# One decode step of 16 attention heads: from split products with 128 stationary columns to plain fp32 products with 32, in column groups of the array

## The chip, the core and the metric

The kernel runs on one core of one Trainium2 chip. The metric is the device time of one execution in microseconds. TensorE (PE) multiplies, with a separate instruction that loads the stationary operand (PEld); VectorE (DVE), ScalarE (ACT) and GpSimd (POOL) do elementwise work; SyncE (SP) issues most transfers.

## The reference, cut to what matters

One layer of a hybrid streaming encoder is computed for a prompt of 512 tokens and for 8 decode sequences of 16 tokens, all in fp32. Head group A has 16 heads of 64. Its decode part, which is what the change touches, is plain attention over a cache of 256 keys and the 16 new ones, with a learned bias by relative distance:

```python
s = jnp.einsum('bgqhrd,bgkhd->bghrqk', q, k) * (HEAD_DIM ** -0.5)
s = s + bias
p = jnp.exp(s - m); denom = jnp.sum(p, axis=-1, keepdims=True)
w = (p / denom).astype(v.dtype)
o = jnp.einsum('bghrqk,bgkhd->bgqhrd', w, v)
```

Around it stand the input projections, the prompt's attention, group B's attention, an output projection and a gated feed-forward network of 2048 x 5632.

## The kernel before, in words

All tokens (512 + 128 = 640) are columns, in two halves of 320. Large products are **dense**: a weight tile of 128 x 128 stays in the array and 320 columns pass through it. An fp32 operand is split into a high part (fp32r, by ACT) and a low rest (by DVE), and a product becomes three: high by high, high by low, low by high (`mm3`, lines 207 to 209 for all callers). Products that stay plain fp32 stand on lines 251 and 263 (row sums and a broadcast for the norms). Transposes are TensorE instructions on line 324.

Attention is written as generators. `decode_a(g)` treats the 8 heads of half g as four pairs of heads; one pair's queries are the 128 rows (two heads of 64). For each of the 8 batch elements b it

1. places the element's queries in `z`, whose other places are zero, so that in the 128 stationary columns of pair t only the 32 columns of that pair (2 heads x 16 tokens) are filled;
2. loads the keys (`cka`), splits them and adds them into one bank with three products for each of four pairs, all accumulating, since the zeros keep the pairs apart: 12 products of 272 columns;
3. adds the bias, takes maximum and exponent (ACT, lines 699 and 700), and loads the values (`cva`);
4. transposes the probabilities of 128 rows (3 transposes), splits them, splits the values and multiplies all 512 value columns by all 128 query rows: 3 x 3 products of 512 columns. Of those 512 columns a row needs only its own head's 64;
5. scales by the denominator, transposes 4 blocks and copies the wanted diagonal blocks out (`diagonal`).

Order of work. `pump` advances one generator by one `yield`; `tick` calls it at a given rate after each step of a dense product (6 matmuls). From the fifth pair of projections on there are two streams, heads of the prompt and `decode` (group B's decode, then `decode_a(0)`), which take turns; `drain_queue("decode")` after the last projection pumps until both parts are done. Then group B's attention outputs are read back and scaled (`group_operands`, lines 202 and 203) as operands of the first output projection, into whose 16 dense products `decode_a(1)` is fed. The number of yields in `decode_a` therefore decides over how many dense steps it spreads. TensorE runs the recorded order (`keep_pace`); other engines' orders come from a scheduler. Buffers S, W and D are slots handed out in turn (`get`, `put`).

Of the kernel before, what the change touches and what calls it, by code (L numbers as in the profile page):

```python
# [7 lines left out]
AF = mybir.ActivationFunctionType  # L8
ALU = mybir.AluOpType
# [4 lines left out]
P = 128  # L14
D = 2048
# [6 lines left out]
NB = 8  # L22
DS = 16
CA = 256
# [17 lines left out]
def f(ap):  # L42
    return ap.bitcast(F32)
# [250 lines left out]
def diagonal(ap, first):  # L294

    return bass.AP(tensor=ap.tensor, offset=ap.offset + first, ap=[list(ap.ap[0]), [160, 4], [1, DS]])


def r(ap):
    return ap.bitcast(F32R)  # L300


def build(nc, tc, io, pools):
    n = Net(nc, tc, io, pools)
    dma = nc.sync.dma_start
# [14 lines left out]
    def dram(name, shape):  # L320
        return pools["dr"].tile(list(shape), F32, tag=name, name=name)

    def tr(out, src):
        nc.tensor.transpose(out, src, n.ident)  # L324
# [12 lines left out]
    oa_d, ob_d = dram("oa_d", (8, P, TOK)), dram("ob_d", (8, P, TOK))  # L337
    sa_d, sb_d = dram("sa_d", (3, P, 8, P)), dram("sb_d", (P, 8, P))
# [14 lines left out]
    first = []  # L353
    for kt in range(KT):
# [10 lines left out]
        own, hl = pair("S")  # L365
# [83 lines left out]
    def flip(blocks, lst):  # L449
        w = P * len(blocks)  # L450
        ps = n.bank()[:, :w]
        for i, src in enumerate(blocks):
            tr(ps[:, P * i:P * i + P], src)
        if w <= HT:
            own = (n.get(lst),)
            hl = pack(own[0], w)
        else:
            own, hl = pair(lst, w)
        n.split(ps, *hl)
        return own, hl  # L460
# [183 lines left out]
        n.put("D", kb0, kb1, vb0, vb1)  # L644

    def decode_a(g):
        o_s, bias, z = n.get("D"), n.get("D"), (n.get("D"), n.get("D"))
        for w in z:
            nc.gpsimd.memset(w, 0.0)
        dma(out=bias[:, :CA + DS], in_=io["bias_d"][g])  # L650
        new, held = [], []
        for i in range(3):
            s, two = n.get("S"), (n.get("D"), n.get("D"))
            sv, hl = sh(s, 4, P), [r(sh(x, 4, P)) for x in two]
            dma(out=sv, in_=sa_d[i, :, 4 * g:4 * g + 4])
            yield
            if i < 2:
                n.split(sv, *hl)
            else:
                ps = n.bank().rearrange("p (a b) -> p a b", a=4)  # L660
                for j in range(4):
                    tr(ps[:, j], sv[:, j])
                n.split(ps, *hl)
            n.put("S", s)
            held.extend(two)
            new.append(hl)
        qh, kh, vh = new
        for b in range(NB):
            own = slice(DS * b, DS * b + DS)
            for e in range(2):  # L670
                zv = r(sh(z[e], 4, 160))
                for rr in range(2):
                    rows = slice(64 * rr, 64 * rr + 64)
                    nc.vector.tensor_copy(zv[rows, :, DS * rr:DS * rr + DS], f(qh[e])[rows, :, own])
            raws = n.get("S"), n.get("S")
            for hf in range(2):
                dma(out=sh(raws[hf], 2, CA), in_=io["cka"][b, g, hf])
            yield
            ps = n.bank()[:, :CA + DS]
            for hf in range(2):  # L680
                ko = n.get("S"), n.get("S")
                kd = [r(sh(x, 2, CA + DS)) for x in ko]
                n.split(sh(raws[hf], 2, CA), kd[0][:, :, :CA], kd[1][:, :, :CA])
                n.put("S", raws[hf])
                for e in range(2):
                    nc.gpsimd.tensor_copy(kd[e][:, :, CA:], f(kh[e])[:, 2 * hf:2 * hf + 2, own])
                yield
                yield
                for j in range(2):
                    t = 2 * hf + j  # L690
                    n.mm3(ps, [r(z[e][:, P * t:P * t + P]) for e in range(2)],
                          (kd[0][:, j], kd[1][:, j]), t == 0, t == 3)
                n.put("S", *ko)
# [5 lines left out]
            nc.scalar.activation(pt[:, :CA], s[:, :CA], AF.Exp, bias=mx, accum_out=den)  # L699
# [12 lines left out]
            yield  # L712
            po = n.bank()
            for j in range(2):
                two, vd = pair("S", 512)
                n.split(raws[j][:, :512], *vd)
                n.put("S", raws[j])
                yield
                yield
                n.mm3(po, cut(p3, P * j, P * j + P), vd, j == 0, False)  # L720
                n.put("S", *two)
            n.mm3(po, cut(p3, 256, 384), [x.rearrange("p a b -> p (a b)") for x in vh], False, True)
            n.put("S", *own3)
            od = n.get("S")
            nc.vector.tensor_scalar(od[:, :512], po, den, None, ALU.mult)
            yield
            yield
            pf = n.bank()
            for t in range(4):
                tr(pf[:, P * t:P * t + P], od[:, P * t:P * t + P])  # L730
            n.put("S", od)
            for rr in range(2):
                rows = slice(64 * rr, 64 * rr + 64)
                nc.vector.tensor_copy(sh(o_s, 4, P)[rows, :, own], diagonal(pf[rows], DS * rr))
        dma(out=oa_d[4 * g:4 * g + 4, :, SP:].rearrange("t p c -> p t c"), in_=sh(o_s, 4, P))
        n.put("D", o_s, bias, *z, *held)


    kf, vf = n.get("F"), n.get("F")
# [18 lines left out]
    ps = n.bank()[:, :P]  # L758
# [38 lines left out]
    for p in range(8):  # L797
        if p < 4:
            project_b(2 * p)
            project_b(2 * p + 1)  # L800
        if p == 4:
            while len(n.lists["Q"]) < 4:
                n.pump()
            n.put("S", kb2, kb3)
            n.move("Q", "D", 4)
            n.put("D", cos, sin)
            n.streams = (("heads 0", "heads"), ("decode", "decode"))
            n.add("decode", decode_b())
            n.add("decode", decode_a(0))
            n.rate = 1.1  # L810
        project_a(p)
# [83 lines left out]
    for i, m in enumerate(m for kt in range(8) for m in (kt, kt + 8)):  # L895
        ps = n.dense([(io["w_out_a"][m], 8)], acts_a)
# [87 lines left out]
    raws, late, kept, kept_own = [], [], {}, []  # L984
# [65 lines left out]
    for i in range(NPAIR):  # L1050
        for src in ("w_gate", "w_up"):
# [4 lines left out]
            start, end = i == 0 and src == "w_gate", i == NPAIR - 1 and src == "w_up"  # L1056
# [269 lines left out]
```

## Time and profile before

| | |
|---|---|
| three runs | 2622.56, 2622.76, 2625.93 us, median 2622.76 |
| profiled execution | span 2619.7 us from first to last instruction; the page gives no other time for it |
| TensorE | busy 98% of the span, clock 0.997 |
| VectorE, ScalarE, GpSimd | 77%, 42%, 25% |
| first and last key load of group A | 470.1 and 773.9 us |

The page's ends of matmuls are modelled and overlap, so the price of a matmul is read from the distance between starts. A row of the groups has the line, engine, operation, output and input by name, shapes and count, then busy time and mean duration, then idle time ahead of it and who ended it.

### The profile page before, as it was taken

What the parts mean: (1) busy time and instruction counts of PE and PEld (TensorE: products, weight loads), DVE (VectorE), ACT (ScalarE), POOL (GpSimd) and SP (SyncE); (2) the same over time, 40 slices, a digit from 0 to 9 for tenths busy, and PEclk for the clock granted to TensorE, in tenths of its full rate; (3) what the DMA queues carried; (4) which work ended last, traced back from release to release, by engine and by line L of the source; (5) the groups of instructions that cost most, each with busy time, mean ns of one, the idle gap of its engine ahead of it and who ended that gap; (6) DMA issues with size and microseconds to landing.
All of it is one profiled execution on the core that took longest, in us unless ns stands there. A gap on an engine that the chain in (4) does not pass through costs nothing.

```text
span 2619.7 us, 45100 instructions
## 1 busy us (share of the span) xinstructions
PE 2565.2 (98%) x17437; PEld 2527.9 (96%) x17437; DVE 2027.7 (77%) x3133; ACT 1101.9 (42%) x1797; POOL 663.8 (25%) x573
## 2 busy tenths in 40 slices
PE   8999999999999999999999999999999899999997
PEld 8999998999899999999999999999999899999996
DVE  5775676766866888788888888888888877777797
ACT  5553444444633644443433333433434333333343
POOL 0000000000301203332333333323324433333353
PEclk9999999999999999999999999999999999999998
DMA  5322232444655433443343343343445865666655
GB/s 172 101 69 91 94 102 86 133 124 130 214 188 185 155 131 122 160 162 126 131 142 126 130 144 123 131 146 120 133 147 176 280 189 157 175 175 169 192 156 176
DMA packets 178678, 383.87 MB, mean 147 GB/s; under 512 B 21856, under 2 KB 74080, under 8 KB 178464
## 3 DMA queue, kind: packets, MB, share of 16 engines
q1 hardware_dynamic: 154128, 326.92, 38.8%
q0 software_dynamic: 23184, 52.77, 7.1%
q8 instruction: 137, 2.24, 0.3%
q10 hardware_dynamic: 1152, 1.31, 0.1%
q14 instruction: 77, 0.63, 0.1%
HBM read 299.61 MB, written 80.58 MB: 145 GB/s over the span
## 4 chain that ended last, share of the span: by engine, by line
PE 85%; DVE 8%; DMA 3%; ACT 2%; issue 2%; POOL 0%; SPq 0%; DVEq 0%; ACTq 0%; POOLq 0%
PE dn L209 18%; PE dn L207 18%; PE dn L208 18%; PE at L207 9%; PE at L208 9%; PE at L209 9%; DVE W L199 2%; PE at L324 2%; DMA W<-w_down 1%; PE at L419 1%; DVE S L973 1%; ACT W L198 1%; PE at L215 1%; PE at L214 1%; ACT S L440 0%
## 5 line engine op out<-in xcount | busy, mean ns | idle before, releaser
L207 PE MATMUL dn<-S,W 128*128 128x320 f32 x3694 | 1152.5, 312 | 5.2 <-ACT S L1027 2.7
L209 PE MATMUL dn<-S,W 128*128 128x320 f32 x3694 | 1144.5, 310 | 6.7 <-DVE W L199 6.3
L208 PE MATMUL dn<-S,W 128*128 128x320 f32 x3694 | 1143.3, 310 | 2.0 <-DVE S L203 1.7
L198 ACT ACTIVATE W<-W 128x1024 fp32r<-128x1024 f32 (+2 forms) x632 | 608.2, 963 | 965.9 <-PE dn L208 542.8
L199 DVE TENSOR_TENSOR W<-W,W 128x1024 fp32r<-128x1024 f32 (+2 forms) x632 | 738.7, 1169 | 81.5 <-ACT W L198 77.6
L209 PEld LDWEIGHTS dn<-S,W 128*128 128x128 f32 x3694 | 694.1, 188 | 10.5 <-DVE W L199 10.1
L207 PEld LDWEIGHTS dn<-S,W 128*128 128x128 f32 x3694 | 694.7, 188 | 9.0 <-ACT S L1027 3.0
L208 PEld LDWEIGHTS dn<-S,W 128*128 128x128 f32 x3694 | 694.4, 188 | 4.1 <-DVE S L203 1.9
L209 PE MATMUL at<-S,W 128*128 128x320 f32 x1594 | 493.5, 310 | 4.9 <-DVE W L199 4.8
L207 PE MATMUL at<-S,W 128*128 128x320 f32 x1594 | 492.8, 309 | 0.5 <-ACT W L198 0.5
L208 PE MATMUL at<-S,W 128*128 128x320 f32 x1594 | 492.5, 309 | 0.0
L954 POOL TENSOR_TENSOR W<-W,W 128x1024 f32<-128x1024 f32 (+2 forms) x75 | 158.9, 2118 | 637.5 <-DVE W L199 453.6
L209 PEld LDWEIGHTS at<-S,W 128*128 128x128 f32 x1594 | 299.2, 188 | 7.3 <-DVE W L199 7.3
L207 PEld LDWEIGHTS at<-S,W 128*128 128x128 f32 x1594 | 299.3, 188 | 0.8 <-ACT W L198 0.8
L208 PEld LDWEIGHTS at<-S,W 128*128 128x128 f32 x1594 | 299.3, 188 | 0.0
L973 DVE TENSOR_TENSOR S<-S,dn 128x320 f32<-128x320 f32 x358 | 163.8, 480 | 65.4 <-PE dn L209 65.0
L963 POOL TENSOR_TENSOR W<-W,W 128x1024 f32<-128x1024 f32 (+2 forms) x75 | 163.6, 2181 | 118.9 <-DVE W L199 113.5
L949 DVE TENSOR_TENSOR W<-W,W 128x1024 f32<-128x1024 f32 (+2 forms) x76 | 124.6, 1640 | 62.8 <-DMA W<-w_down 29.5
L973 DVE TENSOR_TENSOR S<-S,at 128x320 f32<-128x320 f32 x262 | 123.3, 480 | 51.4 <-PE at L209 50.5
L980 POOL DMA_DIRECT2D S<-act_d x161 | 88.0, 547 | 178.6 <-PE dn L209 92.0
L951 DVE TENSOR_TENSOR W<-W,W 128x1024 f32<-128x1024 f32 (+2 forms) x76 | 83.4, 1097 | 61.6 <-DMA W<-w_up 31.4
L1044 DVE TENSOR_TENSOR S<-S,half 128x320 fp32r<-128x320 f32 x147 | 120.0, 837 | 1.9
(162 smaller groups left out, 2223.3 us busy)
## 6 DMA issues: line engine op xcount, KB each, us to landing
S<-act_d POOLq DMA_DIRECT2D x161, 320.0 KB, 3.7
W<-w_gate SPq DMA_DIRECT2D x88, 512.0 KB
W<-w_up SPq DMA_DIRECT2D x88, 512.0 KB
W<-w_in SPq DMA_DIRECT2D x66, 512.0 KB
W<-w_down SPq DMA_DIRECT2D x64, 384.0 KB
act_d<-half SPq DMA_DIRECT2D x147, 160.0 KB
act_d<-S SPq DMA_DIRECT2D x147, 160.0 KB
W<-w_down SPq DMA_DIRECT2D x68, 320.0 KB
```

The source lines that it names most:

```text
L198: self.nc.scalar.activation(hi, src, AF.Identity)
L199: self.nc.vector.tensor_tensor(lo, src, f(hi), ALU.subtract)
L207: mm(out, a[0], b[0], start=first, stop=False)
L208: mm(out, a[0], b[1], start=False, stop=False)
L209: mm(out, a[1], b[0], start=False, stop=last)
L949: nc.vector.tensor_tensor(b12[:, w], b12[:, w], b22[:, w], sub)
L951: nc.vector.tensor_tensor(s6[:, w], b11[:, w], b12[:, w], sub)
L954: eng.tensor_tensor(b11[:, w], b22[:, w], s6[:, w], sub)
L963: eng.tensor_tensor(b21[:, w], b21[:, w], s6[:, w], sub)
L973: add = lambda o, a, b: nc.vector.tensor_tensor(o, a, b, ALU.add)
L980: nc.gpsimd.dma_start(out=r(sh(t, 2, HT)), in_=r(act_d[which, :, j]))
L1044: nc.vector.tensor_tensor(r(src), src, hi, ALU.subtract)
```

## The change

Nothing is split any more in group A's decode. Each pair of heads has a product of its own: 32 stationary columns, in that pair's column group of the array, and its result in 32 partitions of the bank. Scores are four products of 272 columns for each batch element instead of twelve; values are 3 blocks x 4 pairs of 128 columns, the pair's own, instead of nine products of 512; the way back is one transpose instead of four. Operands are plain fp32: keys go from the transfer straight into the product, with the new tokens' keys copied beside them by POOL; the transposed probabilities are copied by ACT. The queries of all 8 elements are placed once, the next element's keys are loaded ahead, and an element has 9 yields instead of 14. 336 split products and 48 transposes go, 256 plain ones come.

```diff
-            for e in range(2):
-                zv = r(sh(z[e], 4, 160))
-                for rr in range(2):
-                    rows = slice(64 * rr, 64 * rr + 64)
-                    nc.vector.tensor_copy(zv[rows, :, DS * rr:DS * rr + DS], f(qh[e])[rows, :, own])
+        def keys(b):
+            own = slice(DS * b, DS * b + DS)
+            out = []
+            for hf in range(2):
+                t = n.get("S")
+                k = sh(t, 2, CA + DS)
+                dma(out=k[:, :, :CA], in_=io["cka"][b, g, hf])
+                nc.gpsimd.tensor_copy(k[:, :, CA:], sh(sk, 4, P)[:, 2 * hf:2 * hf + 2, own])
+                out.append((t, k))
+            return out
...
-            for hf in range(2):
-                ko = n.get("S"), n.get("S")
-                kd = [r(sh(x, 2, CA + DS)) for x in ko]
-                n.split(sh(raws[hf], 2, CA), kd[0][:, :, :CA], kd[1][:, :, :CA])
-                n.put("S", raws[hf])
-                for e in range(2):
-                    nc.gpsimd.tensor_copy(kd[e][:, :, CA:], f(kh[e])[:, 2 * hf:2 * hf + 2, own])
-                yield
-                yield
-                for j in range(2):
-                    t = 2 * hf + j
-                    n.mm3(ps, [r(z[e][:, P * t:P * t + P]) for e in range(2)],
-                          (kd[0][:, j], kd[1][:, j]), t == 0, t == 3)
+            for t in range(4):
+                nc.tensor.matmul(ps[32 * t:32 * t + 32], zs[b // 4][:, b % 4, t], ks[t // 2][1][:, t % 2],
+                                 start=True, stop=True)
...
-            own3, p3 = flip([pt[:, P * j:P * j + P] for j in range(3)], "S")
+            for j in range(3):
+                tr(ps[:, P * j:P * j + P], pt[:, P * j:P * j + P])
+            p3 = n.get("S")
+            nc.scalar.activation(p3[:, :3 * P], ps, AF.Identity)
+            if b + 1 < NB:
+                ks = keys(b + 1)
...
-                n.split(raws[j][:, :512], *vd)
-                n.mm3(po, cut(p3, P * j, P * j + P), vd, j == 0, False)
-            n.mm3(po, cut(p3, 256, 384), [x.rearrange("p a b -> p (a b)") for x in vh], False, True)
+            po = n.bank()[:, :P]
+            for j, v in enumerate((*raws, vh)):
+                for t in range(4):
+                    nc.tensor.matmul(po[32 * t:32 * t + 32], p3[:, P * j + 32 * t:P * j + 32 * t + 32],
+                                     v[:, P * t:P * t + P], start=j == 0, stop=j == 2)
...
-            for t in range(4):
-                tr(pf[:, P * t:P * t + P], od[:, P * t:P * t + P])
+            tr(pf, od[:, :P])
```

How the order moves. TensorE in the middle of the first output projection, before: the value products of one batch element of the second half (`at_8947`, the last two of its three blocks of keys, split, 512 columns) between dense products (`dn`).

```order
L209 MATMUL dn_8886<-S_1398_7803,W_1609_8889 128x320
L207 MATMUL at_8947<-S_1623_8967,S_1618_8943 128x512
L208 MATMUL at_8947<-S_1624_8968,S_1618_8943 128x512
L209 MATMUL at_8947<-S_1623_8967,S_1619_8944 128x512
L207 MATMUL at_8947<-S_1420_7891,S_1618_8943 128x512
L208 MATMUL at_8947<-S_1421_7892,S_1618_8943 128x512
L209 MATMUL at_8947<-S_1420_7891,S_1619_8944 128x512
L207 MATMUL dn_8997<-S_1371_7742,W_1630_8999 128x320
```

The same place now, from the transposes of the probabilities (line 319) to the value products of one element (line 719, 32 rows out, four pairs for each block of keys):

```order
L319 MATMUL at_8303<-cst,S_1450_8266 128x128 x3
L208 MATMUL dn_8284<-S_1264_7377,W_1457_8286 128x320
L209 MATMUL dn_8284<-S_1263_7376,W_1458_8287 128x320
L207 MATMUL dn_8284<-S_1267_7385,W_1457_8286 128x320
L208 MATMUL dn_8284<-S_1268_7386,W_1457_8286 128x320
L209 MATMUL dn_8284<-S_1267_7385,W_1458_8287 128x320
L207 MATMUL dn_8284<-S_1267_7385,W_1457_8286 128x320
L208 MATMUL dn_8284<-S_1268_7386,W_1457_8286 128x320
L209 MATMUL dn_8284<-S_1267_7385,W_1458_8287 128x320
L719 MATMUL at_8327<-S_1451_8272,S_1460_8307 32x128 x4
L719 MATMUL at_8327<-S_1452_8273,S_1460_8307 32x128 x4
L719 MATMUL at_8327<-S_1295_7449,S_1460_8307 32x128 x4
```

All twelve value products of an element now stand in one block, and eight dense ones separate them from the transposes; a block of four score products (line 686) stands alone in the same way between dense ones:

```order
L209 MATMUL dn_8284<-S_1283_7421,W_1458_8287 128x320
L686 MATMUL at_8370<-S_1461_8309,S_1297_7451 32x272 x2
L686 MATMUL at_8370<-S_1462_8312,S_1297_7451 32x272 x2
L207 MATMUL dn_8397<-S_1256_7360,W_1478_8399 128x320
L208 MATMUL dn_8397<-S_1257_7361,W_1478_8399 128x320
```

So there are 32 such blocks in the kernel, none with a dense product inside. The last block of `decode_a(0)` now stands in the 32nd of the 34 projections; before, its work reached past the last one.

More of the change, by code (lines that the diff above doesn't have):

```diff
@@ L291, in sh @@
     return v
-def diagonal(ap, first):
-    return bass.AP(tensor=ap.tensor, offset=ap.offset + first, ap=[list(ap.ap[0]), [160, 4], [1, DS]])
 def r(ap):
@@ L646, in decode_a @@
     def decode_a(g):
-        o_s, bias, z = n.get("D"), n.get("D"), (n.get("D"), n.get("D"))
+        o_s, bias, sk, vh = (n.get("D") for _ in range(4))
+        z = n.get("D"), n.get("D")
+        zs = [sh(x, 4, 4, 32) for x in z]
         for w in z:
-            nc.gpsimd.memset(w, 0.0)
+            nc.gpsimd.memset(w[:, :512], 0.0)
         dma(out=bias[:, :CA + DS], in_=io["bias_d"][g])
[L651 to L655, printed above, removed]
-            yield
[L657 to L666, printed above, removed]
@@ L667, in decode_a @@
-        qh, kh, vh = new
+        sq, sv = n.get("S"), n.get("S")
+        for t, i in ((sq, 0), (sk, 1), (sv, 2)):
+            dma(out=sh(t, 4, P), in_=sa_d[i, :, 4 * g:4 * g + 4])
+        def keys(b):
[8 more added lines that the diff above has]
+            return out
@@ new lines, in decode_a @@
+        yield
+        yield
+        for b4 in range(2):
+            for rr in range(2):
+                rows = slice(64 * rr, 64 * rr + 64)
+                nc.vector.tensor_copy(
+                    zs[b4][rows, :, :, DS * rr:DS * rr + DS],
+                    sh(sq, 4, P)[rows, :, 64 * b4:64 * b4 + 64].rearrange("p t (b s) -> p b t s", b=4))
+        n.put("S", sq)
+        ps = n.bank()
+        for j in range(4):
+            tr(ps[:, P * j:P * j + P], sh(sv, 4, P)[:, j])
+        nc.scalar.activation(vh[:, :512], ps, AF.Identity)
@@ L668, in decode_a @@
+        n.put("S", sv)
+        ks = keys(0)
+        yield
         for b in range(NB):
             own = slice(DS * b, DS * b + DS)
-            for e in range(2):
-                zv = r(sh(z[e], 4, 160))
-                for rr in range(2):
-                    rows = slice(64 * rr, 64 * rr + 64)
-                    nc.vector.tensor_copy(zv[rows, :, DS * rr:DS * rr + DS], f(qh[e])[rows, :, own])
-            raws = n.get("S"), n.get("S")
-            for hf in range(2):
-                dma(out=sh(raws[hf], 2, CA), in_=io["cka"][b, g, hf])
+            yield
@@ L678, in decode_a @@
             yield
             ps = n.bank()[:, :CA + DS]
-            for hf in range(2):
-                ko = n.get("S"), n.get("S")
-                kd = [r(sh(x, 2, CA + DS)) for x in ko]
-                n.split(sh(raws[hf], 2, CA), kd[0][:, :, :CA], kd[1][:, :, :CA])
-                n.put("S", raws[hf])
-                for e in range(2):
-                    nc.gpsimd.tensor_copy(kd[e][:, :, CA:], f(kh[e])[:, 2 * hf:2 * hf + 2, own])
-                yield
-                yield
-                for j in range(2):
-                    t = 2 * hf + j
-                    n.mm3(ps, [r(z[e][:, P * t:P * t + P]) for e in range(2)],
-                          (kd[0][:, j], kd[1][:, j]), t == 0, t == 3)
-                n.put("S", *ko)
+            for t in range(4):
+                nc.tensor.matmul(ps[32 * t:32 * t + 32], zs[b // 4][:, b % 4, t], ks[t // 2][1][:, t % 2],
+                                 start=True, stop=True)
@@ L694, in decode_a @@
+            n.put("S", *(t for t, _ in ks))
             mx, den, d2 = n.small(1), n.small(1), n.small(1)
@@ L709, in decode_a @@
             yield
-            own3, p3 = flip([pt[:, P * j:P * j + P] for j in range(3)], "S")
+            yield
+            ps = n.bank()[:, :3 * P]
+            for j in range(3):
+                tr(ps[:, P * j:P * j + P], pt[:, P * j:P * j + P])
             n.put("S", pt)
[L712 to L715, printed above, removed]
-                n.split(raws[j][:, :512], *vd)
-                n.put("S", raws[j])
-                yield
-                yield
-                n.mm3(po, cut(p3, P * j, P * j + P), vd, j == 0, False)
-                n.put("S", *two)
-            n.mm3(po, cut(p3, 256, 384), [x.rearrange("p a b -> p (a b)") for x in vh], False, True)
-            n.put("S", *own3)
-            od = n.get("S")
-            nc.vector.tensor_scalar(od[:, :512], po, den, None, ALU.mult)
+            p3 = n.get("S")
+            nc.scalar.activation(p3[:, :3 * P], ps, AF.Identity)
+            if b + 1 < NB:
+                ks = keys(b + 1)
             yield
             yield
-            pf = n.bank()
-            for t in range(4):
-                tr(pf[:, P * t:P * t + P], od[:, P * t:P * t + P])
+            po = n.bank()[:, :P]
[3 more added lines that the diff above has]
+                                     v[:, P * t:P * t + P], start=j == 0, stop=j == 2)
+            n.put("S", p3, *raws)
+            od = n.get("S")
+            nc.vector.tensor_scalar(od[:, :P], po, den, None, ALU.mult)
+            yield
+            yield
+            pf = n.bank()[:, :P]
+            tr(pf, od[:, :P])
             n.put("S", od)
@@ L733, in decode_a @@
                 rows = slice(64 * rr, 64 * rr + 64)
-                nc.vector.tensor_copy(sh(o_s, 4, P)[rows, :, own], diagonal(pf[rows], DS * rr))
+                nc.vector.tensor_copy(sh(o_s, 4, P)[rows, :, own],
+                                      pf[rows].rearrange("p (t c) -> p t c", t=4)[:, :, DS * rr:DS * rr + DS])
         dma(out=oa_d[4 * g:4 * g + 4, :, SP:].rearrange("t p c -> p t c"), in_=sh(o_s, 4, P))
-        n.put("D", o_s, bias, *z, *held)
+        n.put("D", o_s, bias, sk, vh, *z)
     kf, vf = n.get("F"), n.get("F")
```

## The prediction

> **What bounds the kernel now.** I read the clock first, then the page's busy row and the chain, then the stretches in which group A is decoded, then single rows.
>
> ```profile
> core 0: 2619.7 us, clock 0.997
> PE 2565.2 (98%) x17437; PEld 2527.9 (96%) x17437; DVE 2027.7 (77%) x3133; ACT 1101.9 (42%) x1797; POOL 663.8 (25%) x573
> PE 85%; DVE 8%; DMA 3%; ACT 2%; issue 2%; POOL 0%; SPq 0%; DVEq 0%; ACTq 0%; POOLq 0%
> ...
> 470.00:650.00 180.00, 178.63 (x1213) 172.29 (x1211) 122.94 (x300) 86.69 (x185) 13.05 (x41) 1.00 0.41 129
> 650.00:700.00 50.00, 43.88 (x276) 39.97 (x277) 42.06 (x99) 37.42 (x78) 17.63 (x22) 0.97 0.61 195
> 700.00:790.00 90.00, 87.91 (x580) 83.29 (x578) 58.71 (x126) 33.00 (x62) 11.12 (x28) 1.00 0.60 199
> ```
>
> The columns of the last three rows are stretch, length, busy time of PE, PEld, DVE, ACT and POOL, granted clock, DMA share, GB/s. TensorE is the bound: full clock, 98% busy, 85% of the chain. Group A's decode lies from 470 to 800 us; it is fed into the gaps of dense products, so what it costs is TensorE time, almost all of it, plus the 6.1 us of idle and the slower clock between 650 and 700 us, where the rest of heads 0 to 7 is emptied out between the last projection and the first output product.
>
> A busy time says nothing of the price of one matmul, because ends are modelled and overlap. I take starts.
>
> ```profile
> 656.57 0.40 PE L207 MATMUL at<-S,S 128*128 128x512 f32 x1
> 656.80 0.39 PE L208 MATMUL at<-S,S 128*128 128x512 f32 x1
> 657.03 0.39 PE L209 MATMUL at<-S,S 128*128 128x512 f32 x1
> ...
> 662.23 0.28 PE L208 MATMUL at<-S,S 128*128 128x272 f32 x1
> 662.35 0.30 PE L209 MATMUL at<-S,S 128*128 128x272 f32 x1
> 662.49 0.29 PE L207 MATMUL at<-S,S 128*128 128x272 f32 x1
> ...
> 670.49 1.80 PE L324 MATMUL at<-cst,S 128*128 128x128 f32 x15
> ...
> L324 PE MATMUL at<-cst,S 128*128 128x128 f32 x461 | 77.2, 278 | 8.2 <-ACT S L699 3.5 <-DMA S<-sa_d 1.5 <-DVE S L625 1.4
> ```
>
> From start to start: 0.23 us for a split product of 512 columns, 0.125 for one of 272. Fifteen transposes take 1.80 us and one lasts 0.28 from issue to landing, so (1.80 - 0.28)/14 = 0.109 each.
>
> **The change part by part.** *Removed.* Per batch element and group (16 of them) 12 split score products, 9 split value products and 3 of 7 transposes. The rows that count the products:
>
> ```profile
> L207 PE MATMUL at<-S,S 128*128 128x512 f32 x48 | 19.3, 402 | 0.8 <-DVE S L199 0.7 <-ACT S L198 0.2
> L208 PE MATMUL at<-S,S 128*128 128x272 f32 x64 | 19.0, 296 | 0.0
> ```
>
> Three lines each: 3 x 64 x 0.125 + 3 x 48 x 0.231 + 48 x 0.109 = 24.0 + 33.3 + 5.2 = 62.5 us of TensorE time.
>
> *Added.* 64 score products (272 columns) and 192 value products (128 columns), plain fp32, 32 stationary columns each. The trace has plain fp32 products only on lines 251 and 263, all with 128 stationary columns:
>
> ```profile
> L263 PE MATMUL at<-cst,sm x60: 222/275/417, 60.1 to 2606.5; 128*128 128x128 f32 x40, 128*128 128x64 f32 x20
> ...
> 2599.35 0.78 PE L263 MATMUL at<-cst,sm 128*128 128x128 f32 x6
> 2599.80 0.33 PE L263 MATMUL at<-cst,sm 128*128 128x64 f32 x2
> 2599.86 0.28 PE L263 MATMUL at<-cst,sm 128*128 128x64 f32 x1
> 2599.94 0.39 PE L207 MATMUL at<-S,W 128*128 128x320 f32 x1
> ...
> 686.04 1.40 PE L251 MATMUL at<-gains,S 128*128 128x1 f32 x12
> 687.30 0.39 PE L209 MATMUL dn<-S,W 128*128 128x320 f32 x1
> ```
>
> The code issues 30 products on line 263 and the trace has 60: a plain fp32 product is two passes, each with its own weight load. Four passes of 128 columns take 2599.35 to 2599.80, 0.111 each; the first pass of 64 columns is followed after 0.06. A split product moves 512 columns in 0.231, so 64 would need 0.03: a plain pass streams at half that rate. One column costs as much as 128 (12 passes in 1.26 us, 0.105), so there the load of 128 stationary columns is what is paid. From the two split rows a column costs (0.231 - 0.125)/240 = 0.44 ns; a pass of 272 columns therefore lies between 0.125 (the split row) and 272 x 0.88 ns = 0.240, and I take 0.240, since the 64-column passes are nearest to that end (64 x 0.88 = 0.057). For 128 columns: 0.06 to 0.113, I take 0.113.
>
> What decides is whether products in different column groups run beside each other. No row has column groups; the nearest are group B's row groups:
>
> ```profile
> 405.43 0.31 PE L209 MATMUL dn<-S,W 128*128 128x320 f32 x1
> ...
> 405.72 0.31 PE L208 MATMUL dn<-S,W 128*128 128x320 f32 x1
> 405.87 0.31 PE L209 MATMUL dn<-S,W 128*128 128x320 f32 x1
> 406.11 0.34 PE L207 MATMUL at<-S,S 64*128 64x144 f32 x2
> 406.28 0.28 PE L208 MATMUL at<-S,S 64*128 64x144 f32 x2
> 406.39 0.28 PE L209 MATMUL at<-S,S 64*128 64x144 f32 x2
> 406.61 0.41 PE L207 MATMUL dn<-S,W 128*128 128x320 f32 x1
> 406.86 0.31 PE L208 MATMUL dn<-S,W 128*128 128x320 f32 x1
> ```
>
> Dense products start 0.147 apart ((405.87 - 405.43)/3). Each x2 row is two products in different halves of the array, and the pair lasts 0.28 to 0.34, hardly longer than one alone: they run together. [...] With 0.01 us between two groups' starts, a block of four score products is five pass lengths, 5 x 0.24 + 0.03 = 1.23 us; the twelve value products are twelve steps of 0.123 and a last pass, 1.59 us. Sixteen times 2.82 is 45.1 us. If every pass stood alone: 128 x 0.24 + 384 x 0.113 = 74.1 us. If four groups ran fully together: 16 x (2 x 0.24 + 0.03 + 3 x (2 x 0.113 + 0.03)) = 20.4 us. [...]
>
> *Changing the shape of the array.* The rows above price it: 0.24 from the last dense product to the first half-array one instead of 0.147 (+0.09), about 0.14 beyond the last pair's streaming before the dense one starts, and 0.25 instead of 0.147 to the second dense one (+0.10). About 0.335 for a block and back; 32 blocks make 10.8 us. It cannot gain; above I see no reason for more than double. [...]
>
> *Off the path.* The splits of keys, values, probabilities and new rows leave ACT and DVE, POOL makes half as many key copies; TensorE's 178.63 of 180 us busy covered them, so I count nothing. SP issues as many transfers as before, with the next element's keys moved ahead of this element's value products; both kernels keep them behind the same weight loads. Two things come nearer to TensorE, and behind a waiting matmul stand all dense ones:
>
> ```profile
>   ACT S L198: 22.6, 11
> ...
> L198 ACT ACTIVATE W<-W 128x1024 fp32r<-128x1024 f32 x406 | 429.3, 1058 | 620.1 <-PE dn L208 375.0 <-PE at L208 218.0 <-issue 14.7
> L198 ACT ACTIVATE S<-at 128x384 fp32r<-128x384 f32 x32 | 15.5, 487 | 9.3 <-PE at L324 9.3
> ```
>
> The first row, from the view of cva, is ACT waiting for value loads, 11 times, 2 us each; with the split gone TensorE itself waits for a late load. And the probabilities' copy: late in the stage the order leaves 8 dense products (1.2 us) between transposes and value products, against 0.28 for the last transpose to land and 0.49 for the copy; a weight split (1.06) in front of it makes it late by about 0.6. I take nothing for both: the splits that stood between a load and its product took longer than the turns that are lost. Bounds: nothing, and 22.6 us.
>
> *The emptying between 650 and 700 us.* The decode takes fewer turns, so group 0's ends inside the 32nd projection and nothing is left to empty. The waits of TensorE that bear on it:
>
> ```profile
> PE at L324 <- ACT S L699: 3.5, 6, 1.6
> PE dn L208 <- DVE S L203: 1.7, 1, 1.7
> PE at L324 <- DMA S<-sa_d: 1.5, 1, 1.5
> ...
> L203 DVE SCALAR_TENSOR_TENSOR S<-S,gains,S 128x640 fp32r<-128x640 f32 x32 | 30.9, 1003 | 11.1 <-ACT S L202 11.0
> L202 ACT ACTIVATE S<-S,gains 128x640 fp32r<-128x640 f32 x32 | 25.7, 821 | 7.3 <-DMA S<-oa_d 5.0 <-DMA S<-xT 1.2 <-PE at L209 0.7
> ```
>
> Of 7.6 us there (6.1 idle, 1.5 by the clock of 0.97) and 3.5 on line 324 I expect 6 back. What is late next is the scaling of group B's outputs (8 x (0.82 on ACT and then 1.00 on DVE)), which has only the last projection, 96 x 0.147 = 14 us, as cover; with the cover gone line 203's wait stays. Bounds: 11 back, or none.
>
> *Sum* against the profiled span: 2619.7 - 62.5 + 45.1 + 10.8 - 6 = 2607.1. The median of the runs is 2622.8, 3.1 above the span, so 2610.
>
> **The rivals.** *The passes do not overlap* (slower). All column groups use the same 128 rows; if the next group's weights can't be loaded or its product not streamed while the last one runs, the price is 74.1: 2622.8 - 62.5 + 74.1 + 10.8 - 6 = 2639. It decides from the point where less than 16.4 of the 29.0 us between 74.1 and 45.1 are gained. For it: no row shows column groups. Against it: in the dense stream a load starts while the product before it, on the same rows, still runs:
>
> ```profile
> 405.73 0.19 PEld L209 LDWEIGHTS dn<-S,W 128*128 128x128 f32 x1
> ```
>
> It starts at 405.73, 0.01 after line 208's product at 405.72. [...]
>
> *Four groups at once*, or passes at the split rate: 2622.8 - 62.5 + 20.4 + 10.8 - 6 = 2585. For it: the pairs of row groups start together. Against it: those had no second pass of the same product between them.
>
> *The gain is eaten by late loads and copies*: overlap as forecast, but 16 x 0.6 = 9.6 us of late copies or up to 22.6 us of late value loads, with 6 back: 2620 to 2633. For it: the row of cva. Against it: before, too, TensorE stood behind those loads, and waited little.
>
> **How the numbers follow.** Forecast 0.48, own range 2602 to 2617; no overlap 0.22; late loads 0.17; four at once 0.13. About 0.2% (5 us) is what a measurement of this kernel tells from no change. Faster: 0.48 + 0.13 and a little of the late loads, 0.63; same, half of the late loads and the forecast's edge, 0.11; slower 0.26. The range reaches from four at once to no overlap, 2585 to 2639; about 0.15 lies beyond its ends.
>
> **What would show it.** In the new trace: two records per column product; starts within a score block 0.24 and 0.01 apart in turn (all 0.24: the first rival; four close together: the second), a block and the way back adding 0.335; PE idle between the last projection and the first output product below 3 us; no long wait at line 719. I am wrong if a pass of 32 stationary columns has a price of its own, or if a block's entry or exit costs several times the row groups' price.

## The result, and the profile after

| | median of the runs | ratio to before, 95% interval |
|---|---|---|
| before, run beside it | 2624.35 us | |
| changed | 2581.47 us (2579.14 to 2582.9) | 0.9839 (0.9826 to 0.9852) |

The kernel is 1.6% faster, about 43 us, where 2610 us was forecast; the result lies 3.5 us below the range. The direction was right, and the rival called *four groups at once* (2585) came close to the time, and below it turns out to be the right mechanism. The same rows as those shown of before, in the same order (cores, busy row, chain by engine, stretches):

```profile
core 0: 2581.1 us, clock 0.994
PE 2531.9 (98%) x17565; PEld 2490.8 (97%) x17565; DVE 1959.5 (76%) x2991; ACT 1061.4 (41%) x1729; POOL 648.8 (25%) x541
PE 87%; DVE 6%; DMA 3%; ACT 2%; issue 1%; SPq 0%; POOL 0%; DVEq 0%; ACTq 0%; POOLq 0%
...
470.00:650.00 180.00, 174.11 (x1355) 163.30 (x1355) 109.58 (x262) 82.33 (x180) 20.73 (x40) 0.99 0.52 165
650.00:700.00 50.00, 49.99 (x388) 46.72 (x387) 26.48 (x73) 19.91 (x45) 4.13 (x13) 0.98 0.59 189
700.00:790.00 90.00, 89.24 (x730) 83.07 (x729) 49.69 (x86) 30.70 (x57) 13.57 (x13) 1.00 0.71 234
```

TensorE is still the bound at 98%, with 128 more matmul records in 33 us less busy time. The idle of 650 to 700 us is gone, but the stretch before it, full before, now has 5.9 us idle.

For the comparisons below I cut the trace by TensorE's records, since the work at both ends is the same in all kernels: the **middle stretch** runs from record 2900 (432 to 433 us) to the 11,400th from the end (871 us in the changed kernel, 913 before). It took 480.2 us before and 439.0 after, 41.2 less; the rest of the execution took 2.6 more. TensorE's idle time in it, as the profile gives it, was 11.3 us before and 8.3 after.

The four score products of one element, and the twelve value products of another, between dense ones (the timeline of the changed kernel; x8 and x24 are two passes of each product, the length runs from the first start to the last end):

```profile
490.87 0.31 PE L208 MATMUL dn<-S,W 128*128 128x320 f32 x1
491.02 0.31 PE L209 MATMUL dn<-S,W 128*128 128x320 f32 x1
491.26 0.67 PE L686 MATMUL at<-S,S 128*32 128x272 f32 x8
491.85 0.42 PE L207 MATMUL dn<-S,W 128*128 128x320 f32 x1
492.11 0.31 PE L208 MATMUL dn<-S,W 128*128 128x320 f32 x1
...
542.78 0.31 PE L209 MATMUL dn<-S,W 128*128 128x320 f32 x1
543.02 0.86 PE L719 MATMUL at<-S,S 128*32 128x128 f32 x24
543.81 0.41 PE L207 MATMUL dn<-S,W 128*128 128x320 f32 x1
544.06 0.31 PE L208 MATMUL dn<-S,W 128*128 128x320 f32 x1
```

From first start to the next dense product: 0.596 and 0.793 us; 1.23 and 1.59 were forecast for the passes alone. The single starts show why, in us from the block's first, rounded to 0.01 (from the records; the timeline groups them):

```
scores, 8 passes   0 .01 .01 .02   .25 .26 .27 .27
values, 24 passes  0 .01 .01 .02   .13 .14 .15 .15   .24 .25 .26 .26
                   .35 .36 .36 .37   .46 .47 .47 .48   .57 .58 .58 .59
```

Four start within 0.02 us, then four more at 0.25 to 0.27 us. The program has the second pass of pair 0 ahead of the first of pair 1; the array did not wait for it.

### The profile page after: what moved, and what is told of

Same layout as the page of the kernel before. It is cut to its first block, busy times and chain, and to the rows that moved or that the text cites. A ratio compares the mean times of both kernels' runs of the same rounds, so it can differ in the third digit from the quotient of the medians.

```text
span 2581.1 us, 45056 instructions
## 1 busy us (share of the span) xinstructions
PE 2531.9 (98%) x17565; PEld 2490.8 (97%) x17565; DVE 1959.5 (76%) x2991; ACT 1061.4 (41%) x1729; POOL 648.8 (25%) x541
## 4 chain that ended last, share of the span: by engine, by line
PE 87%; DVE 6%; DMA 3%; ACT 2%; issue 1%; SPq 0%; POOL 0%; DVEq 0%; ACTq 0%; POOLq 0%
PE dn L207 19%; PE dn L209 19%; PE dn L208 19%; PE at L207 8%; PE at L209 8%; PE at L208 8%; DVE W L199 2%; PE at L319 2%; PE at L414 1%; DMA W<-w_down 1%; DVE S L971 1%; PE at L215 1%; PE at L214 1%; DMA S<-x_d 0%; ACT W L198 0%
```

## The experiments

The theories, in short. **A**: each column group runs its own chain of passes beside the others. **B**: the prediction's block, as long as it would be if starts kept program order. **C**: plain passes are simply cheap, whatever the groups. For the rest of the gain, **D**: fewer turns end the first half's decode before the last projection. **E**: the splits gone from VectorE and ScalarE shortened waits.

### Does the order of the products decide? (x1, then x9)

```diff
-            for j, v in enumerate((*raws, vh)):
-                for t in range(4):
+            for t in range(4):
+                for j, v in enumerate((*raws, vh)):
```

> The changed kernel with the twelve value products of an element written group by group (all three blocks of pair 0, then pair 1, ...) instead of block by block; same products, same operands. Theory A, each column group runs its own products and does not wait for what the program has ahead in another group: a value block stays at about 0.79 us from first start to the next dense start, and the time within 3 us of the changed kernel's 2581.5. Theory B, products start in program order and overlap only with a neighbour: six passes of one group stand behind each other before the next group begins, 21 to 24 steps of 0.113 = 2.4 to 2.7 us a block, 16 x (1.6 to 1.9) = 26 to 31 us more, 2607 to 2612. In between: the order reaches some products ahead, but not six, and the block lies between 0.8 and 2.4 us.

Measured: 2591.5 us, ratio to before 0.9884 (0.9869 to 0.9899); middle stretch 449.3, 10.3 more than changed. The block, in its timeline:

```profile
546.04 1.59 PE L719 MATMUL at<-S,S 128*32 128x128 f32 x24
547.56 0.41 PE L207 MATMUL dn<-S,W 128*128 128x320 f32 x1
```

It takes 1.518 to the dense product instead of 0.793; 16 x 0.725 = 11.6 us. That is neither A (0.79) nor B (2.4 or more). The starts fall into four chains of six passes; the records don't name the group, so the chains are read from the distances:

```
0    .133 .243 .352 .461 .570
.248 .382 .491 .600 .709 .818
.497 .630 .739 .848 .958 1.067
.745 .878 .987 1.097 1.206 1.315
```

Each chain begins about 0.005 us after the *second* product of the chain before it (.243, .491, .739), while that chain's third product still stands waiting. So I formed **F**: a group holds one product (two passes) running and one waiting; only a third one stops what stands behind it. Against **G**: any waiting product stops all behind it. Writing the products two by two tells them apart:

```diff
-            for j, v in enumerate((*raws, vh)):
-                for t in range(4):
+            for j, t in [(j, t) for js in ((0, 1), (2,)) for t in range(4) for j in js]:
```

> The changed kernel with the value products written two by two: blocks 0 and 1 of pair 0, blocks 0 and 1 of pair 1, ..., then the four of block 2. In the kernel written group by group (three products of a pair in a row) the next group began 0.248 us after the one before, just after that group's second product had started, while its third still stood waiting. Theory F, each group holds one product running and one waiting, and only a third one stops what stands behind it: with two in a row all four groups start at once, a value block stays at 0.79 us and the time within 3 us of 2581.5. Theory G, a product that has to wait stops all behind it (program order): each group begins 0.248 after the one before, a block takes about 1.5 us, 16 x 0.73 = 11.6 us more, 2590 to 2593.

Measured: 2581.0 us, 0.9839 (0.9825 to 0.9852), the changed kernel's ratio.

```profile
542.88 0.88 PE L721 MATMUL at<-S,S 128*32 128x128 f32 x24
543.69 0.41 PE L207 MATMUL dn<-S,W 128*128 128x320 f32 x1
```

The block takes 0.812, and its first four starts are 0, .014, .027, .040: twice the spacing, since each chain's second product is passed on between. F holds, G falls.

F can be counted in passes too: in x9 one pass runs and three wait, and nothing is held up; in x1 the next group starts when the third of six passes starts, with three left waiting. The rows of group B in the prediction fit the count in passes: there three split products of one half, a single pass each, are issued in a row, and the other half's first starts 0.01 us behind. Counted in products they would not fit, unless row groups behave otherwise; no run here tells that.

### Is it the groups, or the plain pass? (x2, x3)

```diff
-                nc.tensor.matmul(ps[32 * t:32 * t + 32], zs[b // 4][:, b % 4, t], ks[t // 2][1][:, t % 2],
-                                 start=True, stop=True)
+                nc.tensor.matmul(ps[:32], zs[b // 4][:, b % 4, t], ks[t // 2][1][:, t % 2],
+                                 start=t == 0, stop=t == 3)
```

> The changed kernel with all four score products of an element in one column group, adding into the same 32 rows (so the four pairs' scores are summed into one group's rows and the rest of the attention of group A goes on with those; the work of the other engines on them is done on 32 rows). The products' number and size are as in the changed kernel. Theory A, column groups run beside each other, passes of one group one behind the other at 272 x 0.88 ns = 0.24 us: eight passes take 1.92 us instead of two in a row (0.48), 16 x 1.44 = 23 us more, 2604. Theory C, a plain pass of 32 columns is simply cheap and the groups do not matter: no change, 2581.

This kernel leaves out the separate scores of the four pairs, so it is a measure of time alone. Measured: 2605.8 us, 0.994 (0.9923 to 0.9956); middle stretch 22.5 more than changed.

```profile
535.41 2.02 PE L686 MATMUL at<-S,S 128*32 128x272 f32 x8
537.36 0.41 PE L207 MATMUL dn<-S,W 128*128 128x320 f32 x1
```

In one group the eight passes start 0.229 apart (the first 0.253), 1.95 us to the dense product; 16 x (1.952 - 0.596) = 21.7. A, and not C.

The other side: plain fp32, but as wide as before.

```diff
-                nc.tensor.matmul(ps[32 * t:32 * t + 32], zs[b // 4][:, b % 4, t], ks[t // 2][1][:, t % 2],
-                                 start=True, stop=True)
+                nc.tensor.matmul(ps, z[b % 2][:, P * t:P * t + P], ks[t // 2][1][:, t % 2], start=t == 0, stop=t == 3)
...
+                nc.tensor.matmul(po, p3[:, P * j:P * j + P], v[:, :512], start=j == 0, stop=j == 2)
```

> Operands unsplit as in the changed kernel, but products as wide as before: 128 stationary columns of which 32 are filled for the scores, all 512 value columns by all 128 query rows, four transposes back. It takes the column groups away and leaves the plain fp32. Theory A, the gain is the column groups': an element costs 8 passes of 272 (0.24 each) + 6 of 512 (0.45) + 7 transposes (0.109) = 5.4 us of TensorE instead of 12 x 0.125 + 9 x 0.231 + 0.76 = 4.3 before, 16 x 1.04 = 17 us more than before, less about 5 of shorter stalls: about 2636. Theory C, the gain is that of plain fp32 (a pass at the split product's price, 0.125 and 0.231): 16 x (0.5 + 0.69) = 19 less than before and 5 of stalls, about 2600.

Measured: 2632.0 us, 1.004 (1.0025 to 1.0055).

```profile
544.85 1.99 PE L687 MATMUL at<-S,S 128*128 128x272 f32 x8
...
557.46 2.74 PE L718 MATMUL at<-S,S 128*128 128x512 f32 x6
```

Its passes start 0.229 (272 columns) and 0.429 (512) apart; the first is the same number as with 32 stationary columns. An element costs 8 x 0.229 + 6 x 0.429 + 0.76 = 5.17 us against 4.34 split: 16 x 0.83 = 13.2 more by the products, 11.5 by the middle stretch. The stretch is no clean measure: TensorE's idle in it is 8.2 us instead of 11.3, but 17.1 us of it stand at half clock instead of 3.4. By the price of the products, leaving out the splits alone makes the kernel slower; the column groups make the gain.

### What does a change of the array's shape cost? (x5, x7)

```diff
             for j, v in enumerate((*raws, vh)):
+                if j:
+                    yield
```

> The changed kernel with a turn of dense products between the three blocks of keys of the value products: four column products, dense products, four more, and so on; 32 more changes between 32 and 128 stationary columns, no product more or less. By the new trace's starts a change there and back costs 0.09 in, 0.09 out and 0.105 at the second dense product, 0.285 together: 32 x 0.285 = 9 us more, 2590.5. By the prediction's 0.335: 10.7, 2592. If a change of the array's shape costs nothing of its own: within 2 us of 2581.5.

Measured: 2589.5 us, 0.9876 (0.9861 to 0.9891); middle stretch 8.8 more, with 0.8 less idle. One element stayed whole, so 30 changes were added.

```profile
515.30 0.31 PE L209 MATMUL dn<-S,W 128*128 128x320 f32 x1
515.54 0.43 PE L721 MATMUL at<-S,S 128*32 128x128 f32 x8
515.90 0.42 PE L207 MATMUL dn<-S,W 128*128 128x320 f32 x1
516.15 0.31 PE L208 MATMUL dn<-S,W 128*128 128x320 f32 x1
```

A piece takes 0.356 to the dense product, plus 0.092 more than a dense step at its entry and 0.105 more at the second dense product. Three pieces are 3 x 0.553 = 1.659, one block 0.793 + 0.197 = 0.990: 0.335 for each added change, the prediction's figure to the third digit; 30 of them are 10.0. My 0.285, written before this run, had left out that the passes' end is not covered either.

The other direction puts the next element's scores right behind this element's values:

```diff
                     nc.tensor.matmul(po[32 * t:32 * t + 32], p3[:, P * j + 32 * t:P * j + 32 * t + 32],
                                      v[:, P * t:P * t + P], start=j == 0, stop=j == 2)
+            if b + 1 < NB:
+                ps = scores_of(b + 1, ks)
```

> The changed kernel with the next element's score products moved right behind this element's value products, and the way back one turn later: 18 blocks of column products instead of 32, same products, nine turns for an element still. If a change of the array's shape costs 0.285: 14 x 0.285 = 4 us less, 2577.5; by the prediction's 0.335, 4.7 less. If the blocks' price lies in the passes alone: no change. Where the keys come late for the new place, TensorE waits at the score line, and that shows.

Measured: 2575.4 us, 0.9818 (0.9803 to 0.9833); middle stretch 3.6 less than changed. Blocks of 24 and 8 passes now stand together, 1.251 us to the dense product:

```profile
532.23 0.86 PE L736 MATMUL at<-S,S 128*32 128x128 f32 x24
532.91 0.64 PE L681 MATMUL at<-S,S 128*32 128x272 f32 x8
533.48 0.41 PE L207 MATMUL dn<-S,W 128*128 128x320 f32 x1
```

0.793 + 0.596 - 1.251 + 0.197 = 0.335 once more; 14 times is 4.7. The stretch gained less: the changed kernel's wait of 5.4 us on line 389 is down to 1.1, but a new one of 5.7 us on line 199 (of the kind shown below for x8) stands beside it, and 10.2 us of the stretch are at half clock instead of 6.8.

### Where the rest of the gain comes from (x4, x11)

The changed kernel with the old number of turns, and the kernel before with fewer:

```diff
+            for _ in range(5):
+                yield
```

> The changed kernel with 14 turns for a batch element instead of 9, as before the change: only where its pieces stand between the dense products differs. The products' sum leaves about 4.6 us of the gain to fewer stalls. Theory D, that is the emptying after the last projection, which comes back with the turns: 4 to 6 us more than 2581.5, and TensorE idle 4 to 8 us between 650 and 700 us. Theory E, the splits that left VectorE and ScalarE made the stalls shorter: no change, 2580 to 2583.

Measured: 2580.3 us, 0.9835 (0.9822 to 0.9849); middle stretch 438.9 against 439.0. The waits moved (of those above 0.3 us, 2.7 us stand in 470 to 650 us, 1.5 in 650 to 700, 3.3 from there to 860; changed: 5.9, none, 0.6), and the idle of the whole middle stretch is 9.2 us against 8.3. D falls here.

```diff
-                yield
-                yield
+                yield
```

(One `yield` less in the loop over the two value blocks, one behind line 707 and one behind line 725.)

> The kernel before, split products and all, with 10 turns for a batch element instead of 14 and nothing else changed. The changed kernel got back 7 us more in the decode stage than its products account for, of it 4.5 in waits above 0.3 us; giving it 14 turns changed nothing. Theory D', fewer turns end the first half's decode ahead of the last projection and take the waits between 650 and 700 us away, here too: those waits fall from 7 us to below 3 and the time by 3 to 6 us, to 2617 to 2620. Theory E, the splits that left VectorE and ScalarE did it: no change, 2621 to 2625, and the waits only stand elsewhere.

Measured: 2631.8 us, 1.0031 (1.0019 to 1.0043); middle stretch 10.1 more than before. Its waits of TensorE:

```profile
PE at L324 <- ACT S L699: 7.7, 6, 3.4
PE at L324 <- DVE S L394: 6.2, 1, 6.2
```

Both theories missed: with split operands fewer turns are a loss, and a wait of 6.2 us takes the place of the cluster that they were to remove. D is refuted from both sides: turns alone never gave the gain. That the splits' leaving (E) lets the kernel live with nine turns fits both runs, and x3, unsplit with nine turns but without the column groups, is idle for 8.2 us of the middle stretch, as long as the changed kernel (8.3; before 11.3, x11 17.5). But x3 also loads its keys ahead, and no run isolates the splits. E stays open.

### The new wait at the end of the projections (x6, x8, x10)

The changed kernel's waits of TensorE have one row that grew (before has it with 0.3 us, on line 394 there), and what stands around it in the timeline:

```profile
PE at L319 <- DVE S L389: 5.4, 1, 5.4
...
643.69 2.44 DVE L669 COPY S<-S 64x256 f32<-64x256 f32 x4
646.16 0.82 DVE L389 TENSOR_TENSOR S<-dn,S 128x640 f32<-128x640 f32 x1
...
641.34 0.31 PE L208 MATMUL dn<-S,W 128*128 128x320 f32 x1
647.04 1.11 PE L319 MATMUL at<-cst,S 128*128 128x128 f32 x4 [5.39 <-DVE S L389]
...
648.48 0.47 PE L208 MATMUL dn<-S,W 128*128 128x320 f32 x1
648.75 0.47 PE L209 MATMUL dn<-S,W 128*128 128x320 f32 x1
...
653.34 0.31 PE L208 MATMUL dn<-S,W 128*128 128x320 f32 x1
653.48 0.30 PE L209 MATMUL dn<-S,W 128*128 128x320 f32 x1
```

The last projection's result (line 389) stands on VectorE behind four copies of the second half's queries. Moving them:

```diff
-                nc.vector.tensor_copy(
+                (nc.gpsimd if g else nc.vector).tensor_copy(
```

> The changed kernel with the second half's four query copies on GpSimd instead of VectorE. In the new trace VectorE does them (2.4 us) between the scaling of group B's last output and the last projection's result, for which TensorE waits 5.4 us. If VectorE's queue is what is late there: 2.4 us less, 2579. If the scaling ahead of it (which waits for ScalarE and a transfer) ends last anyway: no change.

Measured: 2576.8 us, 0.9822 (0.9808 to 0.9835); middle stretch 4.7 less than changed.

```profile
PE at L319 <- DVE S L389: 2.6, 1, 2.6
...
644.77 0.66 PE L319 MATMUL at<-cst,S 128*128 128x128 f32 x4 [2.55 <-DVE S L389]
...
645.41 0.30 PE L209 MATMUL dn<-S,W 128*128 128x320 f32 x1
645.55 0.31 PE L207 MATMUL dn<-S,W 128*128 128x320 f32 x1
```

The wait lost 2.8 us, a little more than the 2.4 that the copies took, and more went with it. Behind the wait of 5.39 us dense products start 0.267 apart (648.48 to 648.75), 14 of them, until 652 us; behind the one of 2.55 they start 0.147 apart at once. The long wait had cost a slow clock besides (half clock on record from 645.5 to 652.3 us), 14 x 0.12 = 1.7 us and a little on the transposes. That the clock stayed up in x6 was in part luck, as the last section shows.

> The merged blocks and the query copies on GpSimd together. If both hold and are independent: 4 + 2.4 = 6.4 us less than the changed kernel, 2575. If the idle at the end of the projections moves with the other places of the blocks, only one of the two shows: 2577 to 2579.

Measured: 2574.0 us, 0.9811 (0.9797 to 0.9825); middle stretch 6.3 less than changed. The time is that of the first case, but not for its reason: the idle did move. The wait on line 389 is gone, and TensorE now waits 4.7 us for a weight's low part (line 199), queued on VectorE behind scalings (line 203) that had become slow beside GpSimd's sums, 2.1 us each. The timeline of this kernel:

```profile
633.77 8.39 DVE L203 SCALAR_TENSOR_TENSOR S<-S,gains,S 128x640 fp32r<-128x640 f32 x4
...
633.08 8.40 POOL L281 TENSOR_TENSOR S<-S,S 128x640 f32<-128x640 f32 x4 [0.70 <-ACT S L280]
```

The last kernel takes GpSimd's sums away from there:

```diff
-            n.add_square(ssq, o, t == 0, "S")
+            n.add_square(ssq, o, t == 0, "S", nc.vector if o_d is ob_d else None)
```

> The kernel with merged blocks and the queries on GpSimd, and besides the squares of group B's outputs summed on VectorE (line 281) instead of GpSimd. In the merged kernel's trace the scaling on VectorE (line 203) lasts 2.1 to 2.2 us where GpSimd sums the squares at the same time, 0.9 to 1.0 elsewhere, and TensorE waits 4.7 us for the weight's low part queued behind it (line 199). If GpSimd's sums slow it: line 203 at 0.9 to 1.0 throughout, the wait below 2.5 us though VectorE has eight sums more, 2 to 4 us less than 2574. If not, or if the sums on VectorE take as long as what they save: 2574 or more.

Measured: 2571.4 us, 0.9805 (0.979 to 0.982); middle stretch 429.9, 2.8 less than with merged blocks and copies alone. The ratios of these two can't be told apart.

```profile
634.25 0.87 DVE L203 SCALAR_TENSOR_TENSOR S<-S,gains,S 128x640 fp32r<-128x640 f32 x1
635.05 0.81 DVE L281 TENSOR_TENSOR S<-S,S 128x640 f32<-128x640 f32 x1
635.78 0.88 DVE L203 SCALAR_TENSOR_TENSOR S<-S,gains,S 128x640 fp32r<-128x640 f32 x1
```

Each scaling is back at 0.88, and with seven sums more VectorE is done sooner (the first of the eight is a square only); what is left at that place is a wait of 2.8 us on line 389. Against the changed kernel (0.9839) this version, at 0.9805, is about 0.35% faster, with intervals that don't touch.

## Why the prediction missed

By its own terms, us:

| term | predicted | measured |
|---|---|---|
| split products and transposes removed | -62.5 | -64.9 |
| column-group passes | +45.1 | +17.8 |
| 32 changes of the array's shape | +10.8 | +10.7 |
| the emptying between 650 and 700 us | -6 | -3.1, the idle of the whole middle stretch |
| not placed | 0 | -1.7, what is left of the middle stretch |
| outside the stretch | 0 | +2.6 |

The first row is the sum of the distances from each record's start to the next in the middle stretch, idle left out: 25.4 us for the split products of 272 columns, 34.0 for those of 512, and 23.0 before less 17.4 after for the transposes of line 324 (now 319).

**The step that failed** is the length of a block, five pass lengths (scores) and twelve steps with a last pass (values), of which the +45.1 is made. That length was the author's assumption, and no run shows the +45.1. Measured in its place, without the shape's price: 0.596 + 0.197 - 0.335 = 0.458 us, two passes of 0.229, and 0.793 + 0.197 - 0.335 = 0.655, six of 0.109. Sixteen times 1.113 is 17.8, 27.3 us less, nearly all of the 28.5 between forecast and median. The experiments x1, x9 and x2 show the mechanism: a chain for each group, one plain product waiting in it without holding up the others. That is the rival *four groups at once*, which the prediction priced at 20.4 us and gave a chance of 0.13.

The rows of group B that the prediction quotes could have decided between its three prices: they stand in pairs 207 x2, 208 x2, 209 x2 (at 406.11, 406.28 and 406.39), while the code issues 207, 208, 209 for one half and then for the other. Pairs 0.01 apart had been read as overlap; they were also a changed order. The starts of x1 show a changed order for column groups too: .248 for the second pair, .461 for the third product of the first pair, which the program has ahead of it. The slower rival asked whether one group's weights can be loaded while another's product runs: all column groups use the same 128 rows, and the loads of the score block above are out long before its first passes have streamed:

```profile
491.25 0.16 PEld L686 LDWEIGHTS at<-S,S 128*32 128x32 f32 x8 [0.19 <-issue]
```

Eight loads, of the first and the second passes, begin and end between 491.25 and 491.41, while the second passes start at 491.51. So the loads of these groups did not wait for the passes that ran, and the slower rival is out.

**The pass and the shape** were right. 0.240 and 0.113 were taken, 0.229 and 0.109 found, 32 stationary columns at no price of their own (passes of 272 start 0.229 apart with 32 in x2 and with 128 in x3). 0.335 for a block was exact.

**The emptying** gave back half of what was forecast. The idle between 650 and 700 us is gone, 6.1 us of it, but the new wait on line 389 put 5.4 us just ahead; the idle of the whole middle stretch went from 11.3 to 8.3 us. That turns alone do it, as its sentence has it ("the decode takes fewer turns, so group 0's ends inside the 32nd projection and nothing is left to empty"), is refuted by x4 and x11. "What is late next" was right in place, the end of the projections, but named line 203; it was line 389, queued behind the placing of the queries, an added instruction whose queue the prediction had not walked. **Late loads**: no wait at line 719 appears, and that rival is out.

**Outside the stretch** the changed kernel's profiled execution has 33 dense products at 0.267 (12 near 2000 us, 9 near 2020, 12 near 2540), after waits of 2.75, 2.18 and 1.81 us; the kernel before has waits of the same length there, and its clock stays up behind them. That is 33 x 0.12 = 4.0 us, more than the whole 2.6, and no work of the change.

## What to carry to other kernels

Small products with few stationary columns belong in column groups side by side, issued round robin over the groups (eight passes took 0.596 us here in four groups, 1.952 in one): two plain fp32 products of one group in a row cost next to nothing here (0.02 us a block), three cost 0.25 us for each next group. Gather them in blocks, since each visit between whole-array products costs 0.335 us here, and price unsplit fp32 alone first: without the groups it made this kernel slower (5.17 us an element against 4.34). Where rows show instructions in another order than the program has, that order is a finding about the queue, and it prices the change better than an assumption does.

## What was unexpected of the hardware

- A wait of TensorE had a second price. Behind 5.4 us dense products started 0.267 apart instead of 0.147 for some 5 us, behind 2.55 us (x6) not at all, behind 2.8 us (x10) 12 of them. The granted clock on record changes in steps of 3.41 us (the changed kernel has half clock for 6.83 us from 645.5 and for 3.41 from 2004, 2024 and 2540), and what the traces tie it to is the idle time within one step. Steps around the waits of the changed kernel, x6 and x10 (stretch, length, busy time of PE, granted clock, DMA share, GB/s):

```profile
642.10:645.50 3.40, 0.00 (x0) 1.00 1.00 351
645.50:648.90 3.40, 1.86 (x8) 0.50 0.41 151
...
639.90:643.30 3.40, 2.32 (x16) 1.00 0.88 280
643.30:646.70 3.40, 1.93 (x14) 1.00 1.01 361
...
640.30:643.70 3.40, 1.63 (x10) 1.00 0.84 296
643.70:647.10 3.40, 3.40 (x15) 0.50 0.92 282
```

  In x6 the border between two steps cut the wait into 1.1 and 1.5 us; in x10 1.8 us fell into one step, and the next ran at half clock. In all thirteen traces, from 400 to 2550 us, 32 steps at full clock hold more than 1.75 us of idle, and 31 of them are followed by half clock (the other is in x11, 1.9 us); of the 8118 with less, one is (in the kernel before, 1.1 us). So a wait of one length cost a slow clock or not by where the border fell: 2.75 us near 2000 us in the changed kernel were followed by 3.41 us at half clock, 2.75 us near 2040 in the kernel before by none, with at most 1.74 us of them in one step. About half of a step idle was enough here, 1.8 us.
- VectorE's scaling of 128 x 640 took 2.1 us beside GpSimd's sums (x8) and 0.88 without them (x10).
